# Seven products of quarters in both feed-forward products of a one-layer trunk, with the second one's sums added in DRAM

## Chip, core and metric

The kernel runs on one core of one Trainium2 chip. The metric is the device time of one execution in microseconds (us), given as the median of several runs. Traces come from one more execution, which the hardware profiler recorded.

## What is computed

One layer of a hybrid decoder trunk in float32, for 512 tokens (T) of width 2048. The last line of the layer is what matters here:

```python
x = x + jnp.concatenate([y_a, y_b, y_c], axis=-1) @ w_out[l]
h = rms_norm(x, mlp_norm[l])
x = x + jnp.square(jax.nn.relu(h @ w_mlp_in[l])) @ w_mlp_out[l]
```

`w_mlp_in` (W1) is 2048 x 8192, `w_mlp_out` (W2) 8192 x 2048. The lines before it (a combined projection, three groups of heads) are the same in both kernels.

## The kernel before

**Float32 products.** TensorE takes each float32 factor as a rounded high part and the rest, a low part. A product is three matmuls, high x high, high x low, low x high (`mm3`, L162 to L164 in the profile); the weights stand in the array, 128 x 128 at a time, and 512 tokens stream past. These three are called a triple here. Weights come raw from DRAM (queue of SP); ScalarE casts the high part (`wh`), VectorE subtracts for the low part (`wl`), in `split`, L262 and L263. Three buffers each hold raw, `wh` and `wl`, two pieces are loaded ahead.

**A natural group** (`tr_group`) computes four f-tiles (of 128 columns of the weight) for all tokens: for each of 16 K-tiles four triples, into four banks of PSUM. Six banks serve the main products.

**A seven-product group** (class `Strassen`) computes two f-tiles. The K-tiles, even and odd, the two f-tiles and the two halves of the tokens make 2 x 2 quarters on each side; seven products of sums of quarters replace eight. Each takes eight K-tiles and 256 tokens, high and low side by side: one matmul of 512 columns (`wh` against high and low) and one of 256 (`wl` against high), L845 and L846; such a product is called a pair below, the code of the change calls it double. The weight quarters (`wq`, tags `wq` with five buffers, `raw` with three) are combined on VectorE (`ws`, and in place), the token sums stand ready in `tt`, and the products' results are combined from PSUM in the tile `c` (a single buffer) and written to DRAM (`hd`) by POOL's queue.

**Stages.** Up to 758.6 us: projections, heads, `w_out`; x after it (`x1`) goes to DRAM (`x1d`). Then the first feed-forward product x1 @ W1: a natural group of four f-tiles, 29 seven-product groups, a natural group of two. Its results go to DRAM without ReLU. Then the second product in four chunks of 2048 of its K, each with four natural groups: `hid_tasks` loads the hidden tiles of a chunk, takes ReLU, square and scale on VectorE and splits them into high and low. Chunks alternate between two buffers (`hid`, `xhl`), so that the next chunk is made while one is used. Sums of the four chunks stay in SBUF (`acc`, loaded from `x1d`).

**Order.** `stream` loads pieces two ahead and calls the products; `tasks` (conversions) are run one per step between them. In the second product `ordr` keeps ScalarE's and VectorE's instructions in the order of the program; the order on TensorE is the scheduler's.

Of the kernel before, what the change touches and what calls it, by code (L numbers as in the profile page):

```python
# [15 lines left out]
P = 128  # L16
T = 512
# [23 lines left out]
def trunk_kernel(  # L41
# [91 lines left out]
    ssum = cpool.tile([P, T], F32, name="ssum")  # L133
# [176 lines left out]
    def stat_squares():  # L310
# [4 lines left out]
        nc.vector.reciprocal(out=rbc, in_=ssum)  # L315
# [420 lines left out]

    x1d = [dram.tile([P, T], F32, name=f"x1d{n}") for n in range(KT)]
    hd = [dram.tile([P, T], F32, name=f"hd{n}") for n in range(DFF // P)]

    def open_out(ng):  # L740
        if ng == 0:
            flush()
            close_right("tmpb")
            close_right("sgu")
            o_cm.__exit__(None, None, None)
            mlp["x1"] = open_right("x1")
            mlp["xg"] = mlp["x1"].tile([P, KT, T], F32, name="xg")
        for j in range(4):
# [3 lines left out]
    def close_out(pss, ng):  # L752

        xg = mlp["xg"]
# [11 lines left out]
        if ng == 3:  # L766
# [4 lines left out]
            tasks.append(stat_squares)  # L771
            tasks.extend(lambda m=m, j=j: x_sums(tt, xv, m, j) for m in range(2) for j in range(4))

# [4 lines left out]

    def x_sums(tt, xv, m, j):
# [3 lines left out]
        out, a, b = [(x11, x12, x11), (x12, x22, x12), (x22, x22, x11), (x21, x21, x22)][j]  # L783
        nc.vector.tensor_tensor(out=out, in0=a, in1=b, op=ALU.subtract)
        split(tt[:, j, s, 0], tt[:, j, s, 1], out)

    def x_operand(j, m):

        if j < 3:
            k, t = ((0, 0), (1, 0), (1, 1))[j]  # L790
            return x1v[:, 2 * m + k, t]
        return mlp["tt"][:, j - 3, m]
# [4 lines left out]
    class Strassen:  # L797
# [3 lines left out]
        FACTOR = [0, 1, 5, 3, 4, 2, 6]  # L801

        def __init__(self, c0):
            self.c0, self.pieces, self.open_, self.before_load = c0, range(7), None, None
            self.banks = []

        def load(self, j):
            if j == 0:
                if "spool" not in mlp:
                    flush()  # L810
                    close_right("x1")
                    mlp["spool"] = open_right("quarters")
# [3 lines left out]
                for f, k in ((0, 0), (1, 0), (1, 1), (0, 1)):  # L816
                    if (f, k) == (1, 1):
                        t = wpool.tile([P, KT // 2, P], F32, tag="raw", name=f"wq{i}{f}{k}")
                    else:
                        t = sp.tile([P, KT // 2, P], F32, tag="wq", name=f"wq{i}{f}{k}", bufs=5)  # L820
                    nc.sync.dma_start(out=t, in_=w1[:, k::2, self.c0 + f * P:self.c0 + (f + 1) * P])
                    self.q[f, k] = t
            q = self.q
            if j == 0:
                self.s1, self.s2 = (mlp["spool"].tile([P, KT // 2, P], F32, tag="ws", name=f"ws{n}{self.i}", bufs=2) for n in (1, 2))
                nc.vector.tensor_tensor(out=self.s1, in0=q[1, 0], in1=q[1, 1], op=ALU.add)
            elif j == 1:
                nc.vector.tensor_tensor(out=self.s2, in0=self.s1, in1=q[0, 0], op=ALU.subtract)
            elif j == 2:
                nc.vector.tensor_tensor(out=q[1, 0], in0=q[0, 0], in1=q[1, 0], op=ALU.subtract)  # L830
            elif j == 3:
                nc.vector.tensor_tensor(out=q[0, 1], in0=q[0, 1], in1=self.s2, op=ALU.subtract)
# [6 lines left out]
        def product(self, j, h, l):  # L839
            sp, i = mlp["spool"], self.i  # L840
            pv = main_ps(f"pt{j}{i}").rearrange("p (h t) -> p h t", h=2)
# [6 lines left out]
            def add(out, a, b):  # L848
                nc.vector.tensor_tensor(out=out, in0=a, in1=b, op=ALU.add)

            def take(out, more):
                add(out, pv[:, 0], more)
                add(out, pv[:, 1], out)
# [6 lines left out]
            if j in (0, 3):  # L860
                p = self.p[j // 3]
                nc.scalar.copy(out=p, in_=pv[:, 0])
                add(p, pv[:, 1], p)
# [7 lines left out]
            elif j == 5:  # L871
                take(c[:, 3], c[:, 0])
            elif j == 6:
                take(c[:, 4], c[:, 1])
            if j == 6:
                for n in range(2):
                    nc.gpsimd.dma_start(out=hd[self.c0 // P + n], in_=c[:, 2 + 2 * n:4 + 2 * n].rearrange("p h t -> p (h t)"))  # L877

    def close_mlp_in(pss, f0):

        for j, ps in enumerate(pss):
            if j % 2 == 0:
                cc = mlp["spool"].tile([P, 6, TH], F32, tag="c", name=f"cn{f0 + j}")
            c = cc[:, 2 * (j % 2):2 * (j % 2) + 2]
            ordr(nc.scalar.copy(out=c, in_=ps.rearrange("p (h t) -> p h t", h=2)))
            nc.gpsimd.dma_start(out=hd[f0 + j].rearrange("p (h t) -> p h t", h=2), in_=c)

    def hid_of(c):
        return xhl if c % 2 else mlp["hid"]

    def hid_tasks(c, ks, alloc, ahead):

        room = {}
        d = hid_of(c)

        def load(n):
            if n < len(ks):
                room[n] = alloc(ks[n])
                nc.gpsimd.dma_start(out=room[n], in_=hd[c * KC + ks[n]])

        def rest(n):
            t, k = room.pop(n), ks[n]
# [137 lines left out]
```

## Time and profile before

| | |
|---|---|
| median of 3 runs | 2067.32 us (2066.99 to 2067.97) |
| profiled execution | 2066.59 us, of it the recorded span 2064.9 |
| TensorE busy | 2051.5 us, 99% |
| VectorE busy | 1198.2 us, 58% |
| ScalarE busy | 677.5 us, 33% |
| granted TensorE clock | 0.999 of full |

The span is the part of the execution in which the engines' instructions lie; what lies around it is 1.7 us. Matmuls are pipelined, so a matmul's recorded duration is longer than its share of the time: the step from one start to the next is what counts. An engine's idle time costs something only where TensorE ends up waiting for it.

### The profile page before, as it was taken

The numbers are of one execution on the slowest core, as the hardware profiler recorded it, in microseconds if no ns is written. First come the engines' busy times: TensorE is split into PE (matmuls) and PEld (weight loads), VectorE is DVE, ScalarE is ACT, GpSimd is POOL, SyncE is SP. The second block draws the span as 40 slices with busy tenths as digits, with TensorE's granted clock in tenths as the row PEclk, the third lists the DMA queues.
The fourth block names the chain that finished last, engine by engine and source line by source line (L and its number), as shares of the span: only waits on it lengthen the run. The fifth ranks groups of instructions, "written<-read, shape, count | busy, mean of one in ns | idle before, by whom it ended". The sixth has DMA issues, their size and how long they took to land.

```text
span 2064.9 us, 25736 instructions
## 1 busy us (share of the span) xinstructions
PE 2051.5 (99%) x10274; PEld 1751.2 (85%) x10274; DVE 1198.2 (58%) x1675; ACT 677.5 (33%) x905; POOL 100.6 (5%) x194
## 2 busy tenths in 40 slices
PE   9999999999999999999999999989999999999999
PEld 9999888888888888888888888878888888888888
DVE  5443453534334489899998998866624632652222
ACT  5334442322233443344334333333312321322121
POOL 0000000100000000000000000120100000000000
PEclk9999999999999999999999999999999999999999
DMA  7423222433533454444444344364433432432332
GB/s 248 133 75 108 72 72 69 125 99 97 193 113 123 130 148 141 145 122 141 132 126 148 121 141 128 103 241 156 143 101 108 147 114 100 136 124 95 119 116 82
DMA packets 247016, 259.69 MB, mean 126 GB/s; under 512 B 11748, under 2 KB 179940, under 8 KB 246896
## 3 DMA queue, kind: packets, MB, share of 16 engines
q1 hardware_dynamic: 229888, 206.08, 32.3%
q0 software_dynamic: 14560, 47.75, 6.7%
q10 hardware_dynamic: 2448, 4.23, 0.6%
q8 instruction: 80, 1.31, 0.3%
q14 instruction: 40, 0.33, 0.1%
HBM read 232.81 MB, written 25.19 MB: 125 GB/s over the span
## 4 chain that ended last, share of the span: by engine, by line
PE 71%; issue 26%; POOL 2%; DMA 0%; DVE 0%; ACT 0%; POOLq 0%; DVEq 0%; ACTq 0%
PE pt L162 18%; PE pt L163 18%; PE pt L164 18%; PE pn L162 5%; PE pn L163 5%; PE pn L164 5%; POOL hd L877 1%; PE pt L845 1%; PE pt L846 1%; PE sc L529 0%; PE et L542 0%; PE qt L463 0%; ACT wh L262 0%; DMA acc<-x1d 0%; PE warm L124 0%
## 5 line engine op out<-in xcount | busy, mean ns | idle before, releaser
L263 DVE TENSOR_TENSOR wl<-wr,wh 128x1024 fp32r<-128x1024 f32 (+2 forms) x287 | 321.4, 1121 | 612.3 <-ACT wh L262 574.8
L262 ACT CAST wh<-wr 128x1024 fp32r<-128x1024 f32 (+2 forms) x287 | 277.5, 968 | 710.7 <-PE pt L163 578.7
L162 PE MATMUL pt<-xhl,wh 128*128 128x512 f32 (+1 forms) x912 | 352.6, 387 | 0.0
L163 PE MATMUL pt<-xhl,wh 128*128 128x512 f32 (+1 forms) x912 | 351.6, 386 | 0.0
L164 PE MATMUL pt<-xhl,wl 128*128 128x512 f32 (+1 forms) x912 | 351.5, 385 | 0.0
L845 PE MATMUL pt<-tt,wh 128*128 128x512 f32 x928 | 330.5, 399 | 0.0
L846 PE MATMUL pt<-tt,wl 128*128 128x256 f32 x928 | 260.6, 281 | 0.0
L845 PE MATMUL pt<-xhl,wh 128*128 128x512 f32 x696 | 248.5, 399 | 0.0
L262 ACT CAST wh<-wq 128x1024 fp32r<-128x1024 f32 x145 | 152.3, 1050 | 246.2 <-PE pt L845 233.8
L845 PEld LDWEIGHTS pt<-tt,wh 128*128 128x128 f32 x928 | 174.4, 188 | 43.6
L162 PE MATMUL pt<-hid,wh 128*128 128x512 f32 x512 | 200.4, 391 | 6.9 <-ACT wh L262 6.9
L263 DVE TENSOR_TENSOR wl<-wq,wh 128x1024 fp32r<-128x1024 f32 x145 | 177.1, 1222 | 43.5 <-ACT wh L262 40.9
L162 PEld LDWEIGHTS pt<-xhl,wh 128*128 128x128 f32 x912 | 171.3, 188 | 34.6 <-issue 0.2
L164 PEld LDWEIGHTS pt<-xhl,wl 128*128 128x128 f32 x912 | 171.3, 188 | 34.6
L163 PEld LDWEIGHTS pt<-xhl,wh 128*128 128x128 f32 x912 | 171.3, 188 | 34.2 <-issue 0.2
L163 PE MATMUL pt<-hid,wh 128*128 128x512 f32 x512 | 199.9, 391 | 0.0
L164 PE MATMUL pt<-hid,wl 128*128 128x512 f32 x512 | 198.2, 390 | 0.1
L846 PE MATMUL pt<-xhl,wl 128*128 128x256 f32 x696 | 195.5, 281 | 0.0
L162 PE MATMUL pn<-wh,xhl 128*128 128x384 f32 (+2 forms) x512 | 185.8, 366 | 1.3 <-DVE qn L440 1.3
L163 PE MATMUL pn<-wl,xhl 128*128 128x384 f32 (+2 forms) x512 | 179.4, 350 | 0.0
L164 PE MATMUL pn<-wh,xhl 128*128 128x384 f32 (+2 forms) x512 | 179.3, 350 | 0.0
L846 PEld LDWEIGHTS pt<-tt,wl 128*128 128x128 f32 x928 | 175.3, 189 | 0.0
(203 smaller groups left out, 2571.9 us busy)
## 6 DMA issues: line engine op xcount, KB each, us to landing
wr<-in_w_mlp_out_dram SPq DMA_DIRECT2D x128, 512.0 KB, 3.5
wq<-in_w_mlp_in_dram SPq DMA_DIRECT2D x116, 512.0 KB, 4.1
wr<-in_w_in_dram SPq DMA_DIRECT2D x144, 128.0 KB, 2.4
wr<-in_w_out_dram SPq DMA_DIRECT2D x32, 512.0 KB, 3.5
hd<-c POOLq DMA_DIRECT2D x58, 256.0 KB, 2.6
hs<-hd POOLq DMA_DIRECT2D x56, 256.0 KB, 2.9
wr<-in_w_in_dram SPq DMA_DIRECT2D x24, 512.0 KB, 3.5
wr<-in_w_in_dram SPq DMA_DIRECT2D x31, 384.0 KB, 3.5
```

What stands on the lines that cost most here:

```text
L162: nc.tensor.matmul(ps, lhsT=ah, rhs=bh, start=start, stop=False)
L163: nc.tensor.matmul(ps, lhsT=ah, rhs=bl, start=False, stop=False)
L164: last[0] = nc.tensor.matmul(ps, lhsT=al, rhs=bh, start=False, stop=stop)
L262: ordr(nc.scalar.copy(out=dst_h, in_=src))
L263: ordr(nc.vector.tensor_tensor(out=dst_l, in0=src, in1=dst_h.bitcast(F32), op=ALU.subtract))
L845: nc.tensor.matmul(pv, lhsT=h[:, m], rhs=b, start=m == 0, stop=False)
L846: nc.tensor.matmul(pv[:, 1], lhsT=l[:, m], rhs=b[:, 0], start=False, stop=m == KT // 2 - 1)
L877: nc.gpsimd.dma_start(out=hd[self.c0 // P + n], in_=c[:, 2 + 2 * n:4 + 2 * n].rearrange("p h t -> p (h t)"))
```

## The change

It has five parts.

- **Second product.** Chunk 0 is a natural group (f-tiles 0 to 3), four seven-product groups and a natural group (f-tiles 12 to 15); chunks 1 to 3 are six seven-product groups and a natural group each. The operands are hidden tiles (`hid_factor`): the high and low tiles `xh`, `xl`, or the sums in `tt`. Only the two products on `tt` with numbers 2 and 3 are pairs; the other five take a triple of 256 columns.
- **Sums in DRAM.** A group's result is added onto `x1d` by a POOL DMA with `accum_op` (`finish_out`, `close_mlp_out`); in the last chunk the sum so far is loaded, added on VectorE and written out (`load_sum`, `finish_last`).
- **First product.** Only products 0, 1 and 3 are pairs. Products 5 and 6 share a PSUM bank, and one addition of 512 replaces four of 256.
- **ReLU, square, scale** are done once, in the first product, before the hidden tile is written (`hidden`: VectorE, then ScalarE's Square; `stat_x1` now makes the reciprocal root).
- **Conversion and buffers.** The hidden tiles of the next chunk are converted during the last natural group of a chunk (`both_tasks`), into the same tile `xhl` that this group reads, together with the four sums of each pair of K-tiles into `tt`. The tag `wq` has three buffers, and the quarters (0,1) and (1,1) both take `raw`.

```diff
             for m in range(KT // 2):
-
-                b = x_operand(self.FACTOR[j], m)
-                nc.tensor.matmul(pv, lhsT=h[:, m], rhs=b, start=m == 0, stop=False)
-                nc.tensor.matmul(pv[:, 1], lhsT=l[:, m], rhs=b[:, 0], start=False, stop=m == KT // 2 - 1)
+                start, stop = m == 0, m == KT // 2 - 1
+                bh, bl, both = self.factor(FACTOR[j], m)
+                if double:
+                    nc.tensor.matmul(pv, lhsT=h[:, m], rhs=both, start=start, stop=False)
+                    last[0] = nc.tensor.matmul(pv[:, 1], lhsT=l[:, m], rhs=bh, start=False, stop=stop)
+                else:
+                    mm3(pv[:, half], (h[:, m], l[:, m]), (bh, bl), start, stop)
...
-                    if (f, k) == (1, 1):
+                    if k:
                         t = wpool.tile([P, KT // 2, P], F32, tag="raw", name=f"wq{i}{f}{k}")
                     else:
-                        t = sp.tile([P, KT // 2, P], F32, tag="wq", name=f"wq{i}{f}{k}", bufs=5)
+                        t = sp.tile([P, KT // 2, P], F32, tag="wq", name=f"wq{i}{f}{k}", bufs=3)
...
             elif j == 6:
-                take(c[:, 4], c[:, 1])
...
+                add(c[:, 3:5], pv, c[:, 0:2])
+                self.finish(self, c[:, 2:6].rearrange("p (f h) t -> p f (h t)", f=2))
...
+    def hidden(c, src, rb):
+
+        ordr(nc.vector.scalar_tensor_tensor(out=c, in0=src, scalar=0.0, in1=rb, op0=ALU.max, op1=ALU.mult))
+        ordr(nc.scalar.activation(out=c, in_=c, func=AF.Square))
...
+    def sums(t):
+        q = t.rearrange("p k (h t) -> p (k h) t", h=2)
+        sub(q[:, 0], q[:, 1], q[:, 0])
+        sub(q[:, 1], q[:, 3], q[:, 1])
+        sub(q[:, 3], q[:, 3], q[:, 0])
+        sub(q[:, 2], q[:, 2], q[:, 3])
+        return q
...
+        def even(m):
+            tile_high(2 * m)
+            tile_low(2 * m - 1)
+            if m:
+                kept[m - 1] = sums(room[m - 1])
+                high(mlp["tt"][:, :, m - 1, 0], kept[m - 1])
+
+        def odd(m):
+            tile_high(2 * m + 1)
+            tile_low(2 * m)
+            if m:
+                low(mlp["tt"][:, :, m - 1, 1], kept[m - 1], mlp["tt"][:, :, m - 1, 0])
+                if m + 2 < KC // 2:
+                    room[m + 2] = load_pair(c, m + 2)
...
+    def finish_out(g, c):
+        for n in range(2):
+            nc.gpsimd.dma_start(out=x1d[g.c0 // P + n], in_=c[:, n], accum_op=ALU.add)
...
+    def close_mlp_out(pss, c, f0):
+        for j, ps, t in c_tiles(pss, f"co{c}{f0}"):
+            ordr(nc.scalar.copy(out=t, in_=ps))
+            nc.gpsimd.dma_start(out=x1d[f0 + j], in_=t, accum_op=ALU.add)
...
-            groups.append(tr_group(
-                w2[:, c * KC:(c + 1) * KC, ng * T:(ng + 1) * T], 4, hmov(c),
...
+        for f0 in ([0] if c == 0 else []) + [KT - 4]:
+            if f0:
+                for c0 in range(0 if c else T, f0 * P, 2 * P):
+                    groups.append(Strassen(
+                        src, c0, hid_factor, (2, 3), finish_last if tail else finish_out, begin_last if tail else None,
+                    ))
+            groups.append(tr_group(
+                src[:, :, f0 * P:f0 * P + T], 4, hmov,
```

`c_tiles` gives two f-tiles of a natural group one tile `c`, the same single buffer as the seven-product groups use.

**Where the order changes.** ScalarE of the changed kernel at the end of chunk 0's last natural group (the rows give line, operation, output and input; `wh305j` is the weight of product j of the first seven-product group of chunk 1, `hr` a pair of loaded hidden tiles, `xhl` the tile the group reads, `co` a result tile of the group):

```order
L261 CAST wh3051_13805<-wq30501_13761 128x1024 [waits DMAHW4_49,Activation_49]
L943 CAST xhl_93<-hr304_13752 128x512 [waits DMASW7_49,PE_49]
L943 CAST tt_5757<-hr302_13709 128x4x256 [waits DVE_49]
L943 CAST xhl_93<-hr304_13752 128x512 [waits DMASW0_49,PE_49]
L1042 COPY co0120_13843<-pt291_0_13500 128x512
L1042 COPY co0120_13843<-pt291_1_13501 128x512
L1042 COPY co0122_13848<-pt291_2_13502 128x512 [waits DMASW4_49,DMASW3_49,Activation_49]
L1042 COPY co0122_13848<-pt291_3_13503 128x512
L261 CAST wh3052_13854<-ws2305_13764 128x1024
L884 COPY p0305_13884<-pt0305_13858 128x256 [waits PE_49]
L943 CAST tt_5757<-hr304_13752 128x4x256 [waits DVE_49]
L261 CAST wh3053_13894<-ws1305_13763 128x1024
```

The first wait of `co0122` is for the DMAs that empty `co0120`. In the kernel before, the same engine in chunk 0, with `hs` a loaded hidden tile of the next chunk:

```order
L262 CAST xhl_93<-hs297_12109 128x512 [waits DVE_49]
L262 CAST wh305_12232<-wr305_12231 128x1024 [waits DMAHW5_49,PE_49,Activation_49]
L262 CAST xhl_93<-hs300_12157 128x512 [waits DVE_49]
L262 CAST wh307_12268<-wr307_12267 128x1024 [waits DMAHW6_49,PE_49,Activation_49]
L262 CAST xhl_93<-hs302_12193 128x512 [waits DVE_49]
```

There each weight cast has one tile's cast beside it, and results are not copied by ScalarE; the changed kernel has copies and sums' casts between the weight casts. VectorE of the changed kernel at the same place (`wl` low parts, `c305` the first seven-product group's result, `x4` the four sums):

```order
L784 TENSOR_TENSOR hr302_13709<-hr302_13709 128x256 [waits DVE_49] x4
L784 TENSOR_TENSOR xhl_93<-hr304_13752,xhl_93 128x512 [waits DMASW7_49,Activation_49]
L784 TENSOR_TENSOR tt_5757<-hr302_13709,tt_5757 128x4x256 [waits Activation_49]
L784 TENSOR_TENSOR wq30510_13757<-wq30500_13755,wq30510_13757 128x1024
L262 TENSOR_TENSOR wl3052_13855<-ws2305_13764,wh3052_13854 128x1024 [waits PE_49,Activation_49]
L784 TENSOR_TENSOR xhl_93<-hr304_13752,xhl_93 128x512 [waits DMASW0_49]
L784 TENSOR_TENSOR hr304_13752<-hr304_13752 128x256 [waits DVE_49] x4
L784 TENSOR_TENSOR wq30501_13761<-wq30501_13761,ws2305_13764 128x1024
L262 TENSOR_TENSOR wl3053_13895<-ws1305_13763,wh3053_13894 128x1024 [waits PE_49,Activation_49]
L787 TENSOR_TENSOR c305_13883<-pt1305_13898,p0305_13884 128x256 [waits DMASW4_49,DMASW3_49,DMASW7_49,DMASW0_49,PE_49]
L784 TENSOR_TENSOR tt_5757<-hr304_13752,tt_5757 128x4x256 [waits DVE_49]
```

In the kernel before, VectorE closes that group with four additions into `acc` that wait for TensorE alone:

```order
L950 TENSOR_TENSOR acc_11505<-pt279_0_11815,acc_11505 128x512 [waits PE_49]
L950 TENSOR_TENSOR acc_11505<-pt279_1_11816,acc_11505 128x512 [waits PE_49]
L950 TENSOR_TENSOR acc_11505<-pt279_2_11817,acc_11505 128x512 [waits PE_49]
L950 TENSOR_TENSOR acc_11505<-pt279_3_11818,acc_11505 128x512 [waits PE_49]
```

The last sums and low parts now stand behind weight casts, and the first addition into `c305` behind the DMAs of the closing group. SP in the first product, before and then changed (`wq`, group number, f, k):

```order
L821 DMA wq23410_8351<-in_w_mlp_in_dram 128x8x128 [waits DMAHW2_49,DVE_49]
L821 DMA wq23511_8534<-in_w_mlp_in_dram 128x8x128 [waits DMAHW3_49,DVE_49]
L821 DMA wq23401_8355<-in_w_mlp_in_dram 128x8x128 [waits DMAHW5_49,DMAHW4_49,DVE_49]
L821 DMA wq23500_8530<-in_w_mlp_in_dram 128x8x128 [waits DVE_49]
L821 DMA wq23510_8532<-in_w_mlp_in_dram 128x8x128 [waits DMAHW6_49,DVE_49]
```

```order
L836 DMA wq24410_10801<-in_w_mlp_in_dram 128x8x128 [waits DMAHW3_49,DMAHW2_49,DVE_49]
L836 DMA wq24500_11008<-in_w_mlp_in_dram 128x8x128 [waits DVE_49]
L836 DMA wq24401_10805<-in_w_mlp_in_dram 128x8x128 [waits DMAHW4_49,DVE_49]
L836 DMA wq24511_11012<-in_w_mlp_in_dram 128x8x128 [waits DMAHW5_49,DVE_49]
L836 DMA wq24510_11010<-in_w_mlp_in_dram 128x8x128 [waits DMAHW7_49,DMAHW6_49,DVE_49]
```

The load of quarter (0,1) of a group stood behind the next group's (1,1); now it stands ahead of it, behind the next group's (0,0), and waits for a `raw` buffer.

## Rows read from the trace of the kernel before

**Rows 1.** The page: the span, and the chain that ended last by engine.

```profile
span 2064.9 us, 25736 instructions
...
PE 71%; issue 26%; POOL 2%; DMA 0%; DVE 0%; ACT 0%; POOLq 0%; DVEq 0%; ACTq 0%
```

**Rows 2.** Busy time by stage: window, length, engines (instructions), clock, DMA share, GB/s.

```profile
758.60:1332.40 573.80, 573.80 (x3250) 497.53 (x3249) 516.71 (x691) 228.77 (x263) 34.90 (x65) 1.00 0.44 131
1332.40:2061.40 729.00, 721.89 (x3218) 597.75 (x3216) 329.30 (x393) 177.92 (x200) 41.75 (x78) 1.00 0.38 128
```

**Rows 3.** Line 845, seven-product groups: count, duration (ns, min/median/max), first and last start.

```profile
L845 PEld LDWEIGHTS pt<-tt,wh x928: 187/188/188, 764.2 to 1332.0; 128*128 128x128 f32 x186
L845 PE MATMUL pt<-tt,wh x928: 395/398/403, 764.3 to 1332.1; 128*128 128x512 f32 x186
...
L845 PE MATMUL pt<-xhl,wh x696: 389/398/403, 758.7 to 1329.3; 128*128 128x512 f32 x174
```

**Rows 4.** TensorE at the end: start, duration, instruction, count.

```profile
2056.95 0.39 PE L162 MATMUL pt<-xhl,wh 128*128 128x512 f32 x1
...
2058.31 0.28 PE L162 MATMUL pt<-xhl,wh 128*128 128x256 f32 x1
...
2061.06 0.28 PE L164 MATMUL pt<-xhl,wl 128*128 128x256 f32 x1
```

**Rows 5.** DMA issues: count, KB of each, median us from issue to landing.

```profile
wq<-in_w_mlp_in_dram SPq DMA_DIRECT2D x116, 512.0 KB, 4.1
...
hs<-hd POOLq DMA_DIRECT2D x56, 256.0 KB, 2.9
```

**Rows 6.** ScalarE at the first group's close in the first product; brackets: idle before, releaser.

```profile
756.84 1.27 ACT L885 COPY cn<-pt 128x512 f32<-128x512 f32 x2
...
763.50 1.07 ACT L885 COPY cn<-pt 128x512 f32<-128x512 f32 x2 [3.80 <-DMA hd<-cn]
...
764.72 1.07 ACT L262 CAST wh<-ws 128x1024 fp32r<-128x1024 f32 x1
765.67 1.07 ACT L262 CAST wh<-wq 128x1024 fp32r<-128x1024 f32 x1
```

**Rows 7.** VectorE in a seven-product group of the first product.

```profile
774.08 1.22 DVE L263 TENSOR_TENSOR wl<-wq,wh 128x1024 fp32r<-128x1024 f32 x1
775.22 0.68 DVE L849 TENSOR_TENSOR c<-p,c 128x512 f32<-128x512 f32 x1
776.00 0.88 DVE L849 TENSOR_TENSOR c<-pt,c 128x256 f32<-128x256 f32 x2
...
780.76 0.42 DVE L849 TENSOR_TENSOR c<-pt,c 128x256 f32<-128x256 f32 x1
781.09 1.22 DVE L826 TENSOR_TENSOR ws<-wq,wq 128x1024 f32<-128x1024 f32 x1
```

**Rows 8.** ScalarE, then VectorE, while hidden tiles are converted.

```profile
1335.58 0.62 ACT L262 CAST hid<-hr 128x512 fp32r<-128x512 f32 x1 [2.39 <-DVE hr L904]
1336.10 0.62 ACT L262 CAST wh<-wr 128x512 fp32r<-128x512 f32 x1
...
1336.23 0.69 DVE L263 TENSOR_TENSOR hid<-hr,hid 128x512 fp32r<-128x512 f32 x1 [0.74 <-ACT hid L262]
1336.84 0.68 DVE L263 TENSOR_TENSOR wl<-wr,wh 128x512 fp32r<-128x512 f32 x1
```

**Rows 9.** POOL's DMA issues at the last group's close in the first product.

```profile
1361.90 1.08 POOL L886 DMA_DIRECT2D hd<-cn  x2 [17.53 <-ACT cn L885]
1365.91 1.60 POOL L899 DMA_DIRECT2D hs<-hd  x3 [2.92 <-DMA hd<-cn]
```

**Rows 10.** TensorE near the start of the second product.

```profile
1375.81 0.79 PE L162 MATMUL pt<-hid,wh 128*128 128x512 f32 x1 [4.64 <-ACT wh L262]
1376.40 0.63 PE L163 MATMUL pt<-hid,wh 128*128 128x512 f32 x1
1376.83 0.63 PE L162 MATMUL pt<-hid,wh 128*128 128x512 f32 x1
```

More of the change, by code (lines that the diff above doesn't have):

```diff
@@ L314, in stat_squares @@
         nc.vector.tensor_scalar(out=ssum, in0=ps, scalar1=1.0 / D, scalar2=EPS, op0=ALU.mult, op1=ALU.add)
-        nc.vector.reciprocal(out=rbc, in_=ssum)
+        rsqrt(rbc, ssum, *[mlp["x1"].tile([P, T], F32, tag="sq", name=f"rsb_{n}", bufs=2) for n in "sy"])
     def stat_columns4(spool):
@@ L861, in product @@
                 p = self.p[j // 3]
-                nc.scalar.copy(out=p, in_=pv[:, 0])
-                add(p, pv[:, 1], p)
+                ordr(nc.scalar.copy(out=p, in_=pv[:, 0]))
+                if double:
+                    add(p, pv[:, 1], p)
             elif j == 1:
@@ L881, in close_mlp_in, with c_tiles @@
+    def c_tiles(pss, name):
         for j, ps in enumerate(pss):
             if j % 2 == 0:
[L883 to L902, printed above, removed]
-            ordr(nc.vector.scalar_tensor_tensor(out=t, in0=t, scalar=0.0, in1=t, op0=ALU.max, op1=ALU.mult))
-            ordr(nc.vector.tensor_tensor(out=t, in0=t, in1=rbc, op=ALU.mult))
-            split(d[:, 0, k], d[:, 1, k], t)
-            load(n + ahead)
-        for n in range(ahead):
-            load(n)
-        return [lambda n=n: rest(n) for n in range(len(ks))]
+                cc = mlp["spool"].tile([P, 6, TH], F32, tag="c", name=f"{name}{j}").rearrange("p (f h) t -> p f (h t)", h=2)
+            yield j, ps, cc[:, j % 2]
@@ new lines, in close_mlp_in, with pair, load_pair @@
+    def close_mlp_in(pss, f0):
+        for j, ps, c in c_tiles(pss, f"cn{f0}"):
+            hidden(c, ps, rbc)
+            nc.gpsimd.dma_start(out=hd[f0 + j], in_=c)
+    def pair(name):
+        return mlp["spool"].tile([P, 2, T], F32, tag="hp", name=f"{name}{uid()}", bufs=3)
+    def load_pair(c, m):
+        t = pair("hr")
+        for n in range(2):
+            nc.gpsimd.dma_start(out=t[:, n], in_=hd[c * KC + 2 * m + n])
+        return t
+    def sums(t):
[5 more added lines that the diff above has]
+        return q
@@ new lines, in high, with low, parts_tasks, parts @@
+    def high(dst, src):
+        ordr(nc.scalar.copy(out=dst, in_=src))
+    def low(dst, src, h):
+        sub(dst, src, h.bitcast(F32))
+    def parts_tasks(c):
+        room = [load_pair(c, m) for m in range(3)]
+        s = [slice(2 * m, 2 * m + 2) for m in range(8)]
+        def parts(m):
+            if m < 8:
+                high(xh[:, s[m]], room[m])
+            if m:
+                low(xl[:, s[m - 1]], room[m - 1], xh[:, s[m - 1]])
+                room.append(load_pair(c, (m + 2) % 8) if m < 9 else None)
+        def rest(m):
+            t = room[8 + m]
+            q = sums(t)
+            high(mlp["tt"][:, :, m, 0], q)
+            return q
+        kept = {}
+        def even(m):
+            kept[m] = rest(m)
+        def odd(m):
+            low(mlp["tt"][:, :, m, 1], kept[m], mlp["tt"][:, :, m, 0])
+            if m + 3 < 8:
+                room.append(load_pair(c, m + 3))
+        out = [lambda m=m: parts(m) for m in range(9)]
+        for m in range(8):
+            out.extend([lambda m=m: even(m), lambda m=m: odd(m)])
+        return out
@@ new lines, in finish_out, with load_sum, begin_last, finish_last @@
+    def finish_out(g, c):
+        for n in range(2):
+            nc.gpsimd.dma_start(out=x1d[g.c0 // P + n], in_=c[:, n], accum_op=ALU.add)
+    def load_sum(f0):
+        t = pair("acc")
+        for n in range(2):
+            nc.gpsimd.dma_start(out=t[:, n], in_=x1d[f0 + n])
+        return t
+    def begin_last(g):
+        g.acc = load_sum(g.c0 // P)
+    def finish_last(g, c):
+        add(g.acc, c, g.acc)
+        for n in range(2):
+            nc.gpsimd.dma_start(out=out_v[:, g.c0 // P + n], in_=g.acc[:, n])
```

165 lines of the change are left out of this document (82 added, 83 removed).

## Prediction

> **What bounds the kernel now.** The page comes first: of 2064.9 us, the chain of waits that ended last is to 97% matmuls and their issue [rows 1]. The table by stage says the same with TensorE busy for all of the 573.8 us of the first feed-forward product and 721.9 of the 729.0 of the second, at the full clock [rows 2]. So time comes only from fewer or shorter matmuls, and is lost where TensorE waits. The same rows tell where there is room: VectorE is busy for 516.7 us in the first product, for only 329.3 in the second, ScalarE for 177.9 there. The second product is a plain product, so seven products for eight can still be saved there, and two engines have the time to prepare them. What has to be found out is whether they can do so at the places where one chunk of the hidden tiles replaces the other.
>
> **Matmul prices.** One K-tile of a seven-product quarter is a 512-column and a 256-column matmul now. 1624 of the first kind lie between 758.7 and 1332.1 us [rows 3], 0.3533 us a pair. Two full triples (512 columns) run from 2056.95 to 2058.31: 0.680 us each. The last 24 matmuls, of 256 columns, start between 2058.31 and 2061.06: 23 steps of 0.1196, 0.359 a triple [rows 4]. A triple of 256 columns therefore costs 0.0054 more than the pair it replaces, although it loads a third set of weights: the load takes 0.188 us [rows 3] but lies beside the matmul before.
>
> **Second product.** A pair of f-tiles costs 32 x 0.6805 = 21.78 us today. With seven products, two as pairs and five as triples, it is 16 x 0.3533 + 40 x 0.359 = 20.01. 22 of the 32 pairs change (four in chunk 0, six in each other): **-38.8 us**. **First product.** Four of its seven products become triples: 32 x 0.0057 = 0.18 for each of 29 groups: **+5.2 us**.
>
> **Feeding the first product.** VectorE gets lighter (fewer sums, one 512 addition where four stood), so it no longer matters; the ReLU, the scale and the square add one 1024-wide operation on each of VectorE and ScalarE, covered by that room. What tightens is the buffers: the order of SP shows quarter (0,1) now waiting for a buffer that the previous group's (1,1) leaves, after its last low part. The loop is: that low part 1.22, the load 4.1 [rows 5], the cast 1.07 [rows 6], then VectorE's work until the next such low part. Wide operations start 1.14 us apart, additions from PSUM 0.33 [rows 7], one of 512 columns 0.61 [rows 8]; ten wide ones, that one and four small ones are 13.3. With 0.1 at each of four hand-offs it is 20.1 us against 8 x (3 x 0.3533 + 4 x 0.359) = 19.97 of TensorE. I take 0.13 x 29 = **+4 us**; the bounds are 0 and, with a load 0.6 longer since three quarters now come in one burst, +17. In the second product the same loop lacks the ReLU and is covered.
>
> **The chunk change.** This is the term that decides. The natural group that ends a chunk carries the conversion of the next one: cast and low part of 16 tiles, four sums and their cast and low part for each pair of tiles. The tile it writes is the one being read, so tile k can only be written when TensorE is done with k, and tile 15 at the end, G. Before, the next chunk had a second buffer. Each pair of tiles costs, in the order printed in ACT's and DVE's rows: wl 1.14, low part 0.61, four dependent subtractions at 0.43 (a pair takes 0.88) 1.71, cast of the sums 0.95, a tile's cast 0.52, the weight cast 1.07 [rows 6 to 8]. With a hand-off between the engines (0.03 from 1336.20 to 1336.23 [rows 8], and more the other way) that is 6.1 us around both engines, against 8 triples x 0.68 = 5.44 of TensorE. The pairs fall back 0.65 each, and the weight sums of the first seven-product group come on top, 0.8 each. So at G one low part of weights and two pairs of sums are outstanding. From G: that low part starts at 1.8 us, then a tile's low part and the last but one sums (5.25), on ScalarE their cast (6.4), the last tile's cast (6.9) and two copies of the closing group (8.0). The third copy uses the same single buffer, and stands until both adding DMAs have landed, L later. Behind it on ScalarE stand a fourth copy and the weight cast of product 2 (10.15 + L); then wl 1.14, low part 0.61, the last sums 1.71, their cast 0.95, the cast and low part of product 3's weights 1.07 and 1.14 (16.9 + L), an addition and the last sums' low part, done at 18.5 + L. TensorE has 9.8 us to do in that time: products 0 and 1 (5.7), 2 but its last tile (2.5), some of 3 and 4. It stands for 8.7 + L, at three chunk changes. The group that opens chunk 0 closes in the same way without the conversion: copies 1.1, L, copy and weight cast, against the 5.7 of products 0 and 1, and low parts behind: some 2.1 + L. Together 28.2 + 4L.
>
> L is not in the trace: no DMA adds there. The nearest row is the same buffer before, with a plain write: its two copies end at 758.1 and the next starts at 763.50 [rows 6], 5.4 us, while quarters are loading; at the other place POOL issues at 1361.90 and is released at 1365.91 [rows 9], 4.0. An addition has to read the sum first, which by the rows costs at most a read of 2.9 more [rows 5]: 4.0 to 8.3. I take 6, a write among loads and a little: **+52.2 us** (44 to 61). The Trainium skill, "DMA: Bandwidth & Descriptors", section "Rules for kernel authors", says that an accumulating DMA reads its destination and writes it later; no run here shows it yet, and it speaks for the upper half of these bounds. In the other seven-product groups the adding DMAs have from the last addition to the next group's product 1, about 7 us, before anything waits for them, so there they cost nothing at this L.
>
> TensorE after such a wait runs slowly at first: after 4.64 us idle its matmuls start 0.43 apart instead of 0.227 [rows 10]. Most of that falls into time it waits anyway; **+2 us** for what doesn't (0 to 7).
>
> **What goes.** The second product of before has near its start the wait of 4.64 us and the slow matmuls behind it [rows 10]; its 1024 triples (16 K-tiles, 16 f-tiles, 4 chunks) and the 32 of the first product's last two f-tiles, which the window takes along, would be 718.6 at 0.6805, of 729.0 [rows 2]. Those stalls, **-10 us**, hang on accumulators and hidden tiles loaded at the start, which now come earlier. The end is alike (one addition, one write).
>
> **Sum.** 2064.9 - 38.8 + 5.2 + 4 + 52.2 + 2 - 10 = 2079.5 of span; the profiled execution lies 1.7 over its span, and the median of the runs shown, 2067.32, 0.7 over that execution (2066.59): about 2081.
>
> **Rivals.** A measurement of this kernel can tell some 4 us, 0.2%, from no change.
>
> *The conversion keeps pace.* If VectorE and ScalarE overlap where I add, the pairs stay with TensorE, and at G only tile 15, the last sums and the copies are left. Then a change costs about 1.7 + L in place of 8.7 + L: 21 us less, 2060, and 2052 at L = 4. It decides at a cycle of 5.44 us a pair. For it: I add the six durations as if nothing overlapped, and ScalarE is idle through most of that stage [rows 2]. Against it: both engines take their work in program order, and each row waits for the other engine's row before it. Faster; 25%.
>
> *A little better than that walk.* Two or three of the seven pairs' delay recovered, or L = 4 with an unhindered first product: 2063 to 2071, no measurable change. 10%.
>
> *The adding DMAs are slow.* From L of about 7.7 the additions hold up every seven-product group of chunks 0 to 2 (16 groups), not only the ends, and each is two DMAs among the loads of quarters. L = 10 gives 16 us more at the four ends and up to 2.3 x 16 = 37 in the groups: 2097 to 2134. For it: a write at 5.4 [rows 6] and a read of 2.9 [rows 5] one after the other give 8.3. Against: the stage's transfers keep its DMA engines to 0.38 of their time [rows 2]. 13%.
>
> *The weight loads show.* If a third load were not covered, 2160 more matmuls at 0.188 [rows 3] would add 406 us. The steps of [rows 4], 0.1196 with a load in each, speak against it: 1%. The Trainium skill, "TensorE: Matmul & The Clock Gate", section "The mechanism", says that a weight load overlaps a matmul in flight only where their row groups differ; these are all whole-array loads, and the trace disagrees.
>
> **How the numbers follow.** My forecast, slower through the chunk changes, 2071 to 2095, has 51%; the others are as given. The likeliest is 2081. The range leaves out the slow half of the third rival and the fast end of the first: 2051 to 2108. Faster by over 0.2% is the first rival and a rest: 0.26; within 0.2%: 0.11; slower: 0.63.
>
> **What would show it.** Right: pairs of 0.353 and triples of 0.359 in the steady groups of both products; at each chunk change TensorE idle for 12 to 17 us in a few pieces, released by a ScalarE cast and a VectorE low part; ScalarE standing before its third copy, released by the adding DMA; first-product groups at 20.0 to 20.2 us. Wrong: a chunk change with under 8 us idle (first rival), TensorE waiting for VectorE in every group of the second product behind a DMA (third), or 256-column matmuls farther apart than 0.12.

## The result: 1.55% slower

The changed kernel takes 2099.58 us (median of 4 runs, 2097.24 to 2101.93) against 2067.44 (2066.99 to 2067.97): a ratio of 1.0155, 95% interval 1.0138 to 1.0173. That is slower, as forecast, and inside the range, but by 32 us where the forecast said 14. It lies above the 2071 to 2095 that the forecast itself was given; the range reaches that far only for the fast half of the third rival, whose price is not what the trace shows (below). Of the 53 executions of the kernel before that lie beside these runs and the experiments, two took 2056.4 and 2057.4 us, some 10 less than the rest, and no trace of such a one was kept.

The page of the changed kernel: the span, the engines' busy time, the chain that ended last.

```profile
span 2097.4 us, 30649 instructions
...
PE 2034.8 (97%) x12434; PEld 1836.2 (88%) x12434; DVE 1395.6 (67%) x1846; ACT 820.6 (39%) x1086; POOL 158.0 (8%) x270
...
PE 77%; DMA 8%; DVE 8%; ACT 4%; issue 2%; POOL 0%; SPq 0%; ACTq 0%; DVEq 0%
```

TensorE is busy for 16.7 us less than before and the span is 32.5 longer. In the chain that ended last, 97% were matmuls and their issue [rows 1]; now DMA, VectorE and ScalarE have 20%. The table by stage, with the columns of [rows 2]: the first product (a longer window than before, since it takes in most of the last two f-tiles), the close of chunk 0's opening group, one chunk change, and the last chunk after its change:

```profile
758.60:1356.00 597.40, 597.40 (x4256) 562.09 (x4255) 508.21 (x591) 265.12 (x304) 37.28 (x70) 1.00 0.45 136
1402.00:1432.00 30.00, 18.15 (x92) 15.42 (x91) 18.46 (x26) 9.51 (x13) 7.02 (x12) 0.77 0.48 105
1541.00:1573.00 32.00, 19.17 (x97) 15.74 (x96) 20.52 (x30) 11.97 (x17) 6.83 (x10) 0.79 0.44 99
...
1938.00:2095.00 157.00, 156.09 (x1088) 145.85 (x1087) 107.92 (x120) 50.15 (x56) 12.98 (x24) 1.00 0.43 130
```

The first product and the last chunk have TensorE busy for practically all of the time. In the windows around a close TensorE has 18 to 19 us of 30 to 32, and the clock granted over them falls to 0.77 to 0.79: that is where the time went.

One such change, on TensorE:

```profile
1554.60 0.38 PE L161 MATMUL pt<-xhl,wh 128*128 128x256 f32 x1 [0.50 <-ACT xhl L943]
1565.66 0.80 PE L867 MATMUL pt<-tt,wh 128*128 128x512 f32 x1 [10.68 <-ACT wh L261]
1566.92 0.58 PE L868 MATMUL pt<-tt,wl 128*128 128x256 f32 x1 [0.46 <-DVE wl L262]
1567.30 0.63 PE L867 MATMUL pt<-tt,wh 128*128 128x512 f32 x1
1567.73 0.41 PE L162 MATMUL pt<-xhl,wh 128*128 128x256 f32 x1
1567.94 0.41 PE L163 MATMUL pt<-xhl,wl 128*128 128x256 f32 x1
```

After 11 us without a matmul, steps are 0.43 for a 512-column and 0.21 for a 256-column matmul, as in [rows 10]: the clock granted from 1565.60 to 1569.00 is 0.50, the lower of the two levels (1.2 GHz). What it waited for stands in ScalarE's rows of the same place:

```profile
1554.45 1.06 ACT L1042 COPY co<-pt 128x512 f32<-128x512 f32 x2
1563.60 1.07 ACT L1042 COPY co<-pt 128x512 f32<-128x512 f32 x2 [8.08 <-DMA x1d<-co]
1564.55 1.06 ACT L261 CAST wh<-ws 128x1024 fp32r<-128x1024 f32 x1
...
1569.22 1.05 ACT L943 CAST tt<-hr 128x1024 fp32r<-128x1024 f32 x1 [3.33 <-DVE hr L784]
```

The two first copies end at 1555.51. The third waits for the adding DMAs and starts at 1563.60, 8.1 us later; the weight cast of product 2 stands behind it and ends at 1565.61; TensorE starts at 1565.66. The place in the order was the one printed ahead of the prediction. Over the second product the table of waits (engine and line, what it waited for: us in total, times, longest) has:

```profile
DVE c L787 <- DMA x1d<-c: 50.1, 13, 4.6
ACT wh L261 <- DMA wq<-in_w_mlp_out_dram: 46.5, 13, 4.3
...
PE pt L867 <- ACT wh L261: 42.4, 5, 11.3
...
ACT co L1042 <- DMA x1d<-co: 32.8, 4, 8.7
```

And the DMA issues, as in [rows 5]:

```profile
wq<-in_w_mlp_out_dram SPq DMA_DIRECT2D x88, 512.0 KB, 5.4
...
x1d<-c POOLq DMA_DIRECT2D x32, 256.0 KB, 7.1
...
x1d<-xg POOLq DMA_DIRECT2D x16, 256.0 KB, 2.6
...
x1d<-co POOLq DMA_DIRECT2D x16, 256.0 KB, 4.6
```

A write of 256 KB in the first part of the kernel lands in 2.6 us, an adding one from `c` in 7.1. That median lies between two kinds, since they come in twos: the first of two lands 4.1 us after its issue, the second 7.5 (medians of 16 each).

**Where the 32 us are.** The step from each matmul's start to the next, minus the price of its kind (0.2268 for 512 columns, 0.1198 for 256, 0.2366 and 0.1169 in pairs), summed over a stretch, is what TensorE lost there. It is 9.3 us for both products before, and 74.6 after:

| stretch of the changed kernel | lost, us | the prediction's term |
|---|---|---|
| first product | 0.1 | 4 (feeding) |
| then the opening group of chunk 0, to 1402 us | 0.4 | 0 |
| close of chunk 0's opening group | 16.4 | 8.1 (2.1 + L) |
| three chunk changes | 16.6, 17.2, 17.2 | 14.7 each (8.7 + L) |
| seven-product groups elsewhere | 6.7 | 0 |

### The profile page after: what moved, and what is told of

Same layout as the page of the kernel before. It is cut to its first block, busy times and chain, and to the rows that moved or that the text cites. A ratio compares the mean times of both kernels' runs of the same rounds, so it can differ in the third digit from the quotient of the medians.

```text
span 2097.4 us, 30649 instructions
## 1 busy us (share of the span) xinstructions
PE 2034.8 (97%) x12434; PEld 1836.2 (88%) x12434; DVE 1395.6 (67%) x1846; ACT 820.6 (39%) x1086; POOL 158.0 (8%) x270
## 3 DMA queue, kind: packets, MB, share of 16 engines
q0 software_dynamic: 23712, 67.67, 11.7%
HBM read 237.01 MB, written 37.77 MB: 131 GB/s over the span
## 4 chain that ended last, share of the span: by engine, by line
PE 77%; DMA 8%; DVE 8%; ACT 4%; issue 2%; POOL 0%; SPq 0%; ACTq 0%; DVEq 0%
PE pt L161 16%; PE pt L163 16%; PE pt L162 16%; PE pt L867 10%; PE pn L161 5%; PE pt L868 5%; PE pn L162 5%; PE pn L163 5%; DMA x1d<-c 4%; DVE wl L262 3%; DVE hr L784 2%; DMA wq<-in_w_mlp_out_dram 2%; ACT wh L261 2%; DMA x1d<-co 1%; ACT tt L943 1%
## 5 line engine op out<-in xcount | busy, mean ns | idle before, releaser
L163 PE MATMUL pt<-xhl,wl 128*128 128x256 f32 (+1 forms) x1480 | 493.5, 333 | 3.3 <-DVE wl L262 3.3
L161 PE MATMUL pt<-xhl,wh 128*128 128x256 f32 (+1 forms) x1480 | 493.7, 334 | 1.5 <-ACT xhl L943 1.5
L162 PE MATMUL pt<-xhl,wh 128*128 128x256 f32 (+1 forms) x1480 | 493.4, 333 | 1.1 <-DVE xhl L784 1.1
L261 ACT CAST wh<-wq 128x1024 fp32r<-128x1024 f32 x255 | 267.7, 1050 | 378.5 <-PE pt L162 190.7
L262 DVE TENSOR_TENSOR wl<-wq,wh 128x1024 fp32r<-128x1024 f32 x255 | 311.3, 1221 | 82.0 <-ACT wh L261 81.1
L163 PEld LDWEIGHTS pt<-xhl,wl 128*128 128x128 f32 x1480 | 281.7, 190 | 31.7 <-DVE wl L262 4.5
L162 PEld LDWEIGHTS pt<-xhl,wh 128*128 128x128 f32 x1480 | 281.7, 190 | 28.9 <-DVE xhl L784 1.8
L161 PEld LDWEIGHTS pt<-xhl,wh 128*128 128x128 f32 x1480 | 281.3, 190 | 29.3 <-ACT xhl L943 2.1
L163 PE MATMUL pt<-tt,wl 128*128 128x256 f32 x1048 | 297.6, 284 | 3.8 <-DVE wl L262 3.6
L161 PE MATMUL pt<-tt,wh 128*128 128x256 f32 x1048 | 296.9, 283 | 1.8 <-ACT wh L261 1.8
L162 PE MATMUL pt<-tt,wh 128*128 128x256 f32 x1048 | 296.7, 283 | 0.0
L867 PE MATMUL pt<-tt,wh 128*128 128x512 f32 x584 | 215.1, 408 | 42.4 <-ACT wh L261 42.4
L161 PEld LDWEIGHTS pt<-tt,wh 128*128 128x128 f32 x1048 | 199.8, 191 | 6.4 <-ACT wh L261 3.0
L162 PEld LDWEIGHTS pt<-tt,wh 128*128 128x128 f32 x1048 | 199.9, 191 | 0.0
L867 PEld LDWEIGHTS pt<-tt,wh 128*128 128x128 f32 x584 | 112.7, 194 | 68.3 <-ACT wh L261 44.0
L868 PE MATMUL pt<-tt,wl 128*128 128x256 f32 x584 | 166.8, 287 | 1.9 <-DVE wl L262 1.9
```

Source lines behind the costliest of these rows:

```text
L161: nc.tensor.matmul(ps, lhsT=ah, rhs=bh, start=start, stop=False)
L162: nc.tensor.matmul(ps, lhsT=ah, rhs=bl, start=False, stop=False)
L163: last[0] = nc.tensor.matmul(ps, lhsT=al, rhs=bh, start=False, stop=stop)
L261: ordr(nc.scalar.copy(out=dst_h, in_=src))
L262: ordr(nc.vector.tensor_tensor(out=dst_l, in0=src, in1=dst_h.bitcast(F32), op=ALU.subtract))
L867: nc.tensor.matmul(pv, lhsT=h[:, m], rhs=both, start=start, stop=False)
```

## Experiments

Each kernel ran beside the kernel before on the same chip; ratios are to it, with 95% intervals. e1, e2, e3, e6, e7 and e9 start from the changed kernel and take one suspect each; the others put several together. e2, e3, e5 and e9 leave out part of the computation.

### e1: the closing copies get other buffers

```diff
-        for j, ps, t in c_tiles(pss, f"co{c}{f0}"):
+        for j, ps in enumerate(pss):
+            if j % 2 == 0:
+                cc = pair("co")
+            t = cc[:, j % 2]
             ordr(nc.scalar.copy(out=t, in_=ps))
```

> The closing group's two result tiles come from the three pair buffers instead of the single buffer c, so the third copy no longer waits for the adding DMAs. Theory A (ScalarE stands in order behind the adding DMAs, 7.5 to 8.1 us at each of four closes, and the weight cast of product 2 behind it): the waits of 9 to 11.7 us shrink to 2 to 4, 28 to 33 us less, 2067 to 2072. Rival B (the conversion's backlog on VectorE sets the end of the wait, the copies only fill it): at most 8 us less, 2091 or more.

Measured: 2083.53 us, 1.0088 (1.0060 to 1.0116), 16 us less than the changed kernel, between theory A's 28 to 33 and rival B's 8. Its waits, and ScalarE at the turn from the first to the second group after chunk 0's opening close:

```profile
ACT wh L261 <- DMA wq<-in_w_mlp_out_dram: 64.5, 13, 9.1
...
PE pt L867 <- ACT wh L261: 10.8, 4, 3.3
```

```profile
1437.40 1.04 ACT L261 CAST wh<-wq 128x1024 fp32r<-128x1024 f32 x1 [8.51 <-DMA wq<-in_w_mlp_out_dram]
```

The wait that theory A names is gone (42.4 us of TensorE waiting for that cast have become 10.8), so the copies and the adding DMA set it. But half of the gain is given back behind the closes (by the sum of lost steps introduced above, the closes lose 34.2 us instead of 67.4, the rest 23.3 instead of 7.2): the next group's quarters land late, ScalarE waits 8.51 us for one, and 64.5 us in all where it was 46.5 in the table above. The quarter of that row was issued at 1426.78, when the four adding DMAs had all landed (the last at 1423.81). What runs beside it are six 256 KB loads of hidden tiles (`hr`), issued from 1421.16 to 1425.90: POOL held them back (4.64 and 2.02 us) for adding DMAs to land, since the result tiles now take pair buffers too.

### e2: plain writes instead of adding ones

```diff
-x1d[g.c0 // P + n], in_=c[:, n], accum_op=ALU.add)
+x1d[g.c0 // P + n], in_=c[:, n])
...
-x1d[f0 + j], in_=t, accum_op=ALU.add)
+x1d[f0 + j], in_=t)
```

> The DMAs of the second product write instead of adding, so the sums over chunks are left out. Theory A: the landing falls to that of a plain write in the same place, 4.0 to 5.4 us after the copies against 7.5 to 8.1, so 2 to 4 us less at each of four closes, and the 5 us of late low parts in the groups of seven products go: 13 to 20 us less, 2080 to 2087. Rival C (the reading side costs nothing, the long landing is contention with the weight loads): under 5 us less.

Measured: 2076.20 us, 1.0048 (1.0032 to 1.0064), 23 us less.

```profile
wq<-in_w_mlp_out_dram SPq DMA_DIRECT2D x88, 512.0 KB, 5.2
...
x1d<-c POOLq DMA_DIRECT2D x32, 256.0 KB, 3.2
...
x1d<-co POOLq DMA_DIRECT2D x16, 256.0 KB, 3.5
```

The adding costs 23 us in this kernel, more than the 13 to 20 of theory A: by the sum of lost steps some 18 at the four closes, the rest in the groups, which now run even from the second on (20.05 us each). The landing of the groups' results falls from 7.1 to 3.2, beside weight quarters that land as before (5.4 and 5.2). Rival C, contention alone, allowed under 5 us and falls.

### e3: no conversion at the chunk changes

```diff
-            tasks.extend(both_tasks(c + 1))
+            pass
```

> The conversion of chunks 1 to 3 is left out, they use the hidden tiles and sums of chunk 0. Theory A: three closes are left with two copies, the adding DMAs, two copies and a weight cast after the group's end (about 1.1 + 8 + 2.1) against 5.7 us of matmuls, so 5 to 6 us of wait instead of 15 to 17: about 30 us less, 2069. Rival B (the backlog of the conversion sets the wait): all of it goes at three closes, 45 to 48 us less, 2052 to 2055. If the conversion did not matter: no change.

Measured: 2064.23 us, 0.9990 (0.9979 to 1.0002), 35 us less. The first chunk change has one wait left:

```profile
1554.40 0.50 PE L867 MATMUL pt<-tt,wh 128*128 128x512 f32 x1 [2.21 <-ACT wh L261]
```

At a close the adding DMAs start behind the conversion. Taking away the conversion gives 35 us, taking away the adding 23; no run takes away both, so how far the two add up is not shown. The 5 to 6 us that theory A left at each change were 3.5, 5.6 and 3.2, and 2064 lies between its 2069 and rival B's 2055.

### e4: the sums' low part a step later

The low part of a pair's sums moves from `odd(m)` into `even(m + 1)`, ahead of the next sums; e1's buffers are kept.

> As e1, and the low part of each pair's sums is taken one step later, so that VectorE does not stand for ScalarE's cast of the same sums (1.0 to 1.1 us a pair) in the three chunk changes. Theory A: the conversion then keeps nearer to TensorE and the backlog at the end shrinks by 4 to 6 us at three chunk changes: 12 to 18 us below e1, 2050 to 2060. If VectorE's own work (5.2 us a pair against 5.44) and not the wait is the limit: within 4 us of e1.

Measured: 2116.11 us, 1.0247 (1.0223 to 1.0272). Both theories were wrong about this one. ScalarE in the first chunk change:

```profile
1533.03 1.05 ACT L943 CAST tt<-hr 128x1024 fp32r<-128x1024 f32 x1 [4.22 <-DVE hr L784]
...
1540.30 1.05 ACT L943 CAST tt<-hr 128x1024 fp32r<-128x1024 f32 x1 [4.08 <-DVE hr L784]
...
1556.28 1.06 ACT L1050 COPY co<-pt 128x512 f32<-128x512 f32 x2
1564.72 1.07 ACT L1050 COPY co<-pt 128x512 f32<-128x512 f32 x2 [7.37 <-DMA x1d<-co]
```

The sums' casts are 7.27 us apart: the moved operation now stands in the loop wl, low part, low part of sums, sums, cast, weight cast, in place of beside it. And it keeps its pair buffer longer, so that one buffer is left for both result tiles: the third copy waits 7.37 us for the adding DMA again. By accident it is in part e1's test reversed: at the three chunk changes, where the wait is back, 19.8 to 20.3 us are lost (8.4 in e1), at the opening close, where it is not, 9.3 (9.0 in e1). How much of that is the wait and how much the longer loop is not separated.

### e5: e1 and e2 together

> e1's buffers and e2's plain writes together; sums over chunks are left out. e1 took 7.5 us from each of the four waits and lost half of it 20 us later, on quarters that landed late. Theory A (the adding DMAs hold the DMA engines, about 3.5 us for each against some 1 us for a write, and the quarters queue behind four of them): with plain writes that loss is gone, and what e2 had left of the four waits falls from 6.7 to about 3: 2058 to 2063. Rival D (the loss is the same backlog of VectorE and ScalarE, which only reaches TensorE later): the quarters are late here too, 2068 to 2076.

Measured: 2062.61 us, 0.9979 (0.9967 to 0.9991), as theory A has it and not rival D.

```profile
ACT wh L261 <- DMA wq<-in_w_mlp_out_dram: 17.0, 4, 5.4
...
PE pt L867 <- ACT wh L261: 10.8, 4, 3.3
```

The waits for quarters fall from e1's 64.5 to 17.0 us. The closes lose 34.2 us as in e1, the rest 3.2 instead of 23.3. What e1 lost was the adding DMAs' time, not the engines' backlog. But the way is not quite theory A's: the one quarter issued among the four DMAs of chunk 0's opening close landed after 6.1 us instead of 10.1, and when the three behind it were issued, four of the six loads of hidden tiles had landed (the first goes at 1418.54, not 1421.16); those three landed after 5.6 to 5.9 instead of 7.7 to 10.6.

### e6: the sums' cast a step later

```diff
             if m:
                 kept[m - 1] = sums(room[m - 1])
-                high(mlp["tt"][:, :, m - 1, 0], kept[m - 1])
...
             tile_high(2 * m + 1)
+            if m:
+                high(mlp["tt"][:, :, m - 1, 0], kept[m - 1])
```

> ScalarE casts the sums of a pair one step later, after the next tile's cast; nothing else differs from the changed kernel. By the walk, the loop wl, low part, sums, cast, weight cast loses one tile's cast (0.52 us) and goes from 6.1 to 5.6 us a pair, near TensorE's 5.44: 3 to 4 us less at three chunk changes, 2087 to 2092. If the last sums end no sooner or the closing copies set the end alone: no change.

Measured: 2090.30 us, 1.0114 (1.0099 to 1.0129), 9 us less, as theory A has it. In its trace the first casts of sums stand 5.79 us apart in a chunk change where they stood 6.13, the last ones 6.93 as before. The third copy of the first change waits 6.62 us for the adding DMA where it waited 8.08, so the shorter loop is only part of the gain.

### e7: load, add on VectorE, write

The groups of seven products in chunks 0 to 2 use `begin_last`, and a finish that adds on VectorE and writes to `x1d` without `accum_op`.

> In chunks 0 to 2 the groups of seven products load the sum so far, add it on VectorE and write it plainly, as the last chunk does already; the natural groups still add by DMA. Theory A: the last chunk's even groups (20.05 us) appear in chunks 0 to 2 as well, where the late low parts cost 5 us in sum; the four closes stay: 4 to 8 us less, 2092 to 2096. If the second addition and the loads crowd VectorE and the queues: as much or more than now.

Measured: 2094.22 us, 1.0129 (1.0114 to 1.0144), 5 us less.

### e8: e1, e6 and e7 together

> e1, e6 and e7 together. Theory A with independent parts: 16 us (e1), some 10 (e6) and some 5 (e7) less: 2066 to 2071, level with the kernel before. If the parts remove one and the same wait: near e1, 2080. If the loads late behind four adding DMAs were e1's loss and more loads add to it: above 2080.

Measured: 2067.60 us, 1.0000 (0.9991 to 1.0010): level with the kernel before. The parts add up (16 + 9 + 5 = 30 of the 32 us): within some 2 us the three losses are independent, and none hides another.

### e9: chunk 0's sums left out of its opening group

The loop that appends the sums' steps in `parts_tasks` is dropped, and with it the second load of the hidden tiles that they read.

> Chunk 0's sums are not made in its opening group (its products 2 to 6 take what the sums' tile held from the first product); nothing else differs from the changed kernel. My prediction priced that group's close as one without conversion, 2.1 + L; with L = 7.5 from the trace that is 9.6 us, and the trace has 16.5. Theory A (the sums of chunk 0, which the order puts into this group, are the difference): 6 to 8 us less, 2091 to 2094. If the wait there comes from the copies and the adding DMAs alone: no change.

Measured: 2088.41 us, 1.0104 (1.0091 to 1.0118), 11 us less, more than the 6 to 8 of theory A. TensorE at that close:

```profile
1410.12 0.28 PE L163 MATMUL pt<-xhl,wl 128*128 128x256 f32 x1
1412.77 0.79 PE L867 MATMUL pt<-tt,wh 128*128 128x512 f32 x1 [2.37 <-ACT wh L261]
```

ScalarE there copies the results as soon as TensorE has them, and then waits for the adding DMA alone:

```profile
1402.64 1.27 ACT L1040 COPY co<-pt 128x512 f32<-128x512 f32 x2 [2.57 <-PE pt L163]
1410.69 1.07 ACT L1040 COPY co<-pt 128x512 f32<-128x512 f32 x2 [6.78 <-DMA x1d<-co]
```

TensorE's step of 2.65 us there was 9.13 in the changed kernel, and it loses 6.1 us in all at this close instead of 16.4. The sums, with their loads, were the difference.

### e10: the cast in two halves

On e8's kernel, and also in chunk 0, where the cast moves a step later as in e6:

```diff
+    def sums_high(m, q):
+        for h in range(0, 4, 2):
+            high(mlp["tt"][:, h:h + 2, m, 0], q[:, h:h + 2])
...
-                high(mlp["tt"][:, :, m - 1, 0], kept[m - 1])
+                sums_high(m - 1, kept[m - 1])
```

> As e8, with each pair's cast of sums in two halves, the first beside the last two subtractions, also in chunk 0. VectorE stands 0.5 us a pair for that cast in e8, and a pair takes 5.79 us there against TensorE's 5.44; with halves 5.4. Theory A: no more falling back, 2 to 3 us less at three chunk changes and as much in chunk 0: 2056 to 2062, faster than before. If VectorE's work at the end, not the falling back, is left: no change from e8.

Measured: 2056.74 us, 0.9950 (0.9937 to 0.9964): by the medians faster than both kernels, 43 us less than the changed one.

```profile
1545.36 0.50 PE L867 MATMUL pt<-tt,wh 128*128 128x512 f32 x1 [1.19 <-ACT wh L261]
```

```profile
ACT wh L261 <- DMA wq<-in_w_mlp_out_dram: 30.1, 6, 7.2
...
PE pt L867 <- ACT wh L261: 8.6, 7, 2.8
```

The wait for product 2's weight cast at the first change is 1.19 us, where it was 10.68. The first pairs of tiles now take 5.44 us each in that change (the sums' casts start that far apart), as long as TensorE's matmuls.

### e11: the last two copies a product later

On e10's kernel, the third and fourth result are copied at the start of product 1.

> As e10, and the closing group's third and fourth result are copied and added one product later, so that product 2's weight cast stands 1.4 us earlier and the four adding DMAs do not come in one run. Theory A: 1.4 us less at each of four closes, and the quarters behind the DMAs land 2 to 4 us sooner: 2046 to 2054. If the late quarters of the next group set the end anyway: within 4 us of e10.

Measured: 2063.58 us, 0.9985 (0.9976 to 0.9994), 7 us slower than e10, where 3 to 10 less were expected: a miss.

```profile
1540.80 1.07 ACT L261 CAST wh<-ws 128x1024 fp32r<-128x1024 f32 x1
1547.57 1.07 ACT L1054 COPY co<-pt 128x512 f32<-128x512 f32 x2 [5.71 <-DMA x1d<-co]
```

The third copy waits 5.71 us for an adding DMA again. By the code, a pair of sums for the next group (`acc`, loaded from 1540.65) comes ahead of it and takes the third pair buffer, so that the late results share one buffer with the first. The wait was moved, not avoided.

## Why the prediction was right in direction and half the size

**Matmul prices: right.** The first product's groups take 19.98 us where they took 19.78 (from one group's first copy `p` to the next), so 0.20 x 29 = 5.8 for the predicted 5.2. The last chunk's groups take 20.05, for 20.01. Together 33.6 us were to be saved; the span grew by 32.5 while 65.3 more were lost, so 32.8 were.

**Feeding the first product: too dear.** The loop of 20.1 us was priced at 4, and TensorE lost 0.1 there. The quarters landed in 4.1 by the median, as before. (The bound of +17 is a slip: a load 0.6 longer adds 17 to these 4.)

**The chunk change: mechanism right, L short.** The loop was to take 6.1 us a pair, and 0.8 more with the next group's weight sums; ScalarE's casts of sums stand 6.13 us apart, the last ones 6.93. The walk from G held too: product 2's weight cast was to end at 10.2 + L after G. The first matmul of product 0 is at 1547.30, the cast ended at 1565.6, and with L = 8.1 that is it. L was taken as 6 from bounds of 4.0 to 8.3; it is 7.5 (1413.62 to 1421.08), 8.1, 8.6 and 8.7, above the bounds at two of the four closes. That is 5.4 us of the error, half clock included. e1 and e11 show that this wait sets the end of the change: without it the closes lose half as much, and where another edit brings it back, time is lost again.

**The step that failed: the opening close of chunk 0.** The prediction says that it "closes in the same way without the conversion: 2.1 + L". ScalarE at that close:

```profile
1405.28 1.05 ACT L943 CAST tt<-hr 128x1024 fp32r<-128x1024 f32 x1 [4.33 <-DVE hr L784]
1406.23 1.04 ACT L261 CAST wh<-wq 128x1024 fp32r<-128x1024 f32 x1
1411.60 1.05 ACT L943 CAST tt<-hr 128x1024 fp32r<-128x1024 f32 x1 [4.33 <-DVE hr L784]
1412.56 1.06 ACT L1042 COPY co<-pt 128x512 f32<-128x512 f32 x2
1421.08 1.07 ACT L1042 COPY co<-pt 128x512 f32<-128x512 f32 x2 [7.46 <-DMA x1d<-co]
1422.04 1.06 ACT L261 CAST wh<-ws 128x1024 fp32r<-128x1024 f32 x1
```

Casts of sums (`tt`) stand up to the copies, waiting for VectorE, and the first copy is at 1412.56 although TensorE was done with the group some 8 us earlier (product 0 begins at 1404.34). `parts_tasks` splits the tiles in the stage before, but makes the four sums of each pair in this group, for all eight pairs. So it closes behind the sums' part of a conversion: 16.4 us for 8.1. e9 takes the sums out and the close costs 6.1. With e9's own L of 6.8 the formula gives 8.9, so it was also 2.8 too much for what it meant to describe: the terms it lists (3.2 + L against 5.7) make L - 2.5, and the 4.6 added for low parts were not worked out. The sums are the largest part of the error, 8 us.

**The second step that failed: "there they cost nothing".** In the seven-product groups the adding DMAs were to be hidden for about 7 us. VectorE and TensorE in the second group of chunk 0:

```profile
1447.07 1.22 DVE L262 TENSOR_TENSOR wl<-ws,wh 128x1024 fp32r<-128x1024 f32 x1
1452.14 0.42 DVE L787 TENSOR_TENSOR c<-pt,p 128x256 f32<-128x256 f32 x1 [3.85 <-DMA x1d<-c]
1452.48 1.22 DVE L262 TENSOR_TENSOR wl<-wq,wh 128x1024 fp32r<-128x1024 f32 x1
```

```profile
1452.33 0.28 PE L162 MATMUL pt<-tt,wh 128*128 128x256 f32 x1
1453.75 0.39 PE L163 MATMUL pt<-tt,wl 128*128 128x256 f32 x1 [1.13 <-DVE wl L262]
```

The first addition into `c` waits for the DMA that empties it, and the next low part stands behind it; TensorE waits 1.13 us. The table of waits has 50.1 us of this in 13 waits, mostly covered, 6.7 not. Here it was not only L that was short: from the last addition of a group to the first of the next, which is at product 1, pass 5.1 us in e2, where hardly anything waits (median of 13), and not 7. So the DMAs would have been waited for at L = 6 too. This is the third rival's mechanism in 13 of its 16 groups, but at some 0.5 us each where that rival had 2.3; e7 removes the wait and gains 5 us.

**The whole error.** In the span it is 17.9 us (2097.4 for 2079.5). The opening close gives 7.8 of it, the three changes 5.4 (half clock included in both), the groups 6.7, the opening group before its close 0.4, the matmuls 0.8 and the stalls of before 0.7 (they were 9.3 for 10); the feeding takes 3.9 away.

**The first rival** (the conversion keeps pace) did not happen: a pair takes 6.13 us where it needed 5.44. e10 shows what it is worth with the wait for the adding DMAs gone as well: a change loses 4.6 to 5.4 us. **The weight-load rival** is out: the first product lost 0.1 us at 0.359 a triple of 256 columns, each with three loads of 0.188. The Trainium skill, "TensorE: Matmul & The Clock Gate", section "The mechanism", says that a weight load overlaps matmuls in flight only where the row groups differ; by that these loads would not have been covered, and the trace disagrees. (The same section also lets a load into the background weight buffer go ahead of them, which fits the trace.) The adding DMAs from `c` land in 7.1 us where plain ones take 3.2. By the Trainium skill, "DMA: Bandwidth & Descriptors", section "Rules for kernel authors", an accumulating DMA reads its destination and writes it later; the longer landing fits that, but no run shows the reading itself (both pages count 237.01 MB read from DRAM).

Open: e10 still loses 29.7 us by the same sum, mostly in the first two groups of each chunk, and which part of that the four natural closes' adding DMAs cost there was not tried. Nor was the half clock after a wait measured by itself.

## What to carry to other kernels

When work is put into the gaps of a stage, price the place where that work must end, with every task that the order really puts there, not what a function's name suggests; here one group held the sums of a whole chunk, and I had priced it without a conversion. A buffer that an engine fills in program order turns a DMA's landing into that engine's stall, and everything queued behind waits too: give the last results another buffer, and check which loads then wait for that one. Here the saved matmuls outweighed the losses only when the loop that prepares the operands, counted around both engines, was no longer than TensorE's 5.44 us a pair (for the first pairs 5.44 in e10, 5.79 in e8).

## What the runs showed of the hardware

An adding DMA of 256 KB takes POOL 1.03 us to issue (median of 32), a plain one 0.54 in the same line of e2. Two adding DMAs issued at 1555.33 and 1555.90 landed 3.9 and 7.6 us later, two plain ones at the same place in e2 2.3 and 3.3. So the second adding one landed 4.3 us after the first, the second write 1.5. The page counts 23712 packets on the queue `q0` of the changed kernel and 20640 in e2, for the same 67.67 MB: 64 more for each of the 48 adding DMAs.
